# Expert weights fetched with two neighbouring rows per partition, and the features permuted to match

## The chip, the cores and the metric

The kernel runs on one core of one Trainium2 chip. The metric is the device time of one execution in microseconds; the median of three runs of the kernel before is 2015.76 us (2014.58 to 2028.83).

## What is computed

The reference is a two-layer backbone over 512 latent tokens and 256 context tokens of width 1024, all in float32. Each layer is a token mixer (an mLSTM in layer 0, a retention in layer 1) followed by a mixture of 16 experts. Everything is modulated by six vectors per layer that come from the condition `c` (shift, scale and gate of the mixer, shift, scale and gate of the experts). For this case the expert half matters:

```
h   = rmsnorm(x, norm_ffn_g[i]) * (1 + scale) + shift
aff = softmax(h @ router)                       # [tokens, 16]
gate, idx = top_k(aff.T, cap)                   # cap = 64 latent tokens, 32 context tokens
xs  = h[idx]
hid = silu(xs @ w_gate[e]) * (xs @ w_up[e])     # three 1024 x 1024 weights per expert
x  += gate_vector * scatter_add(idx, (hid @ w_down[e]) * gate)
```

Layer 0 does this for latent and context tokens, layer 1 for the latent tokens alone. The output is the latent stream after a final norm. The experts' weights of both layers are 2 x 16 x 3 matrices of 4 MB, about 403 MB of the 544 MB that the kernel reads.

## The kernel before

The kernel is one program written in a tile framework. A matrix product contracts over partitions: 1024 features are cut into 8 blocks of 128, and block k of the activations (the stationary operand, loaded into TensorE by a weight load) meets block k of the rows of the weights (the moving operand). In the traces "out<-moving,stationary" names them in this order.

**Expert weights.** `Route.load` (L1138 to L1158) brings 256 rows of a weight, 1 MB, into one slot of shape 128 x 2 x 1024: partition p holds row p and row p + 128 of the block, two pieces of 4 KB each. `Route.slot` hands out 19 slots or so in turn (four of a common pool and the pools that the mixer has left). All these loads are issued by SyncE's queue (SP), each as soon as the slot's last reader is done. `Route.prefetch` brings the first eight slots while the mixer's output projection runs. The last expert of layer 1 has its down weights in pieces of 2 KB.

**Experts.** `moe` runs over the experts: `gate_up` multiplies the chosen tokens `xs` with the gate weights and the up weights (PSUM tiles `gl` and `ul` for latent tokens, `cg` for context tokens), ScalarE and VectorE make the hidden values `hid` from them, `turn` (L1399) transposes `hid` with TensorE into `hp` and ScalarE copies it to `hT`, and `down` multiplies with the down weights into `y`. All products are in `prod` (L1260). `prep` and `prep_first` transpose the chosen tokens into `xs` (`xp`); in layer 1 they are picked by a product with one-hot columns (`xr`), and two experts are handled together and added back to the token tiles by a product (`back`).

**Vectors.** `ada_set`, `ada_set_lat` and `ada_columns` compute the modulation vectors as columns `modcol`, one feature block per column; `mk_gsc` makes the norm's scale from them; `rowbc` and `gate_rows` turn the mixer's gate and the experts' gate back into rows on all partitions. `mixer_end` does the output projection, the residual, the transposes `ht` of the new tokens (in `residual`, L942) and the router's product; `rt` holds the router's weights. At the start, small vectors are loaded as rows by ScalarE's queue and transposed into the columns `vc1` and `vc2`.

**Order.** The order of the instructions on each engine is not simply that of the program text. The framework's planner lays them out when the program is built, by its own estimates of how long each instruction and transfer takes, except where the code takes an engine out of its hands (`manual_schedule`, as for TensorE in the first and the last expert of layer 1). Once built, the order is fixed: an engine that waits for one instruction holds all that is queued behind it. The change touches no line that sets an order by hand.

Of the kernel before, what the change touches and what calls it, by code (L numbers as in the profile page):

```python
# [9 lines left out]
F32 = mybir.dt.float32  # L10
# [13 lines left out]
NE = 16  # L24
# [20 lines left out]
def backbone(ctx, tc, x, c, ctx_in, c_ctx, ada_w, ada_b, norm_mix_g, norm_ffn_g, final_norm_g,  # L45
# [29 lines left out]
    vc1 = consts.tile([128, 88], F32, name="vc1")  # L75
    vc2 = consts.tile([128, 96], F32, name="vc2")
    cst = consts.tile([128, 8, 32], F32, name="cst")
    with tc.tile_pool(name="ps0", bufs=1, space=PS, reuse_waits="tile") as ps0, \
            tc.tile_pool(name="rows0", bufs=1, reuse_waits="tile") as rows0:
        V = rows0.tile([128, 2, 128], F32, name="V")  # L80
        V1, V2 = V[:96, 0, :], V[:96, 1, :]
# [13 lines left out]
        rows(V1, 16, norm_ffn_g, 0, 16)  # L95
        rows(V1, 32, ada_b, 0, 48)
        rows(V1, 80, final_norm_g, 0, 8)
        rows(V2, 0, ada_b, 6 * D, 48)
        rows(V2, 48, conv_b, 0, 8)
        rows(V2, 56, conv_w, 0, 40)  # L100
        for V, n, vc in ((V1, 88, vc1), (V2, 96, vc2)):
            p = ps0.tile([128, 96], F32, name="pv", bufs=2)
            nc.tensor.transpose(p[:, :n], V[:n, :], ident[:n, :n])
            nc.vector.tensor_copy(vc, p[:, :n])
    conv_bc = vc2[:, 48:56]

    def conv_wc(w, ch):
        return vc2[:, 56 + w * 8 + ch:57 + w * 8 + ch]

    def adab(l):  # L110
        return vc1[:, 32:80] if l == 0 else vc2[:, 0:48]

# [6 lines left out]
    def ada_set(l, s, psp, sbp, wait=0):  # L119
        """modulation vectors 2 s and 2 s + 1 of layer l, both streams, as columns"""  # L120
# [10 lines left out]
    def ada_columns(l, s, acc, psp, sbp, streams, wait):  # L131
# [4 lines left out]
        for cc in range(4):  # L136
            nc.tensor.transpose(tp[:, cc, :], row[:, cc * 128:(cc + 1) * 128], ident)
        src = tp.rearrange("p c (q w) -> p q c w", w=32)
        for v in streams:
            nc.vector.tensor_tensor(modcol[l][:, s * 16:(s + 1) * 16, v].rearrange("p (q c) -> p q c", c=4),  # L140
                                    src[:, :, :, v],
                                    adab(l)[:, s * 16:(s + 1) * 16].rearrange("p (q c) -> p q c", c=4), op=OP.add)
# [5 lines left out]
    def ada_set_lat(l, s, psp, sbp, accs, wait):  # L148
        """ada_set for the latent stream alone; accs: two tiles [128, 1024] for the sums on every partition"""
# [19 lines left out]
    def ada_first(hh, psp, sbp):  # L169
        """shift and scale of the first mixer for half of the features; a column of the weights loaded third"""  # L170
# [18 lines left out]
        for v in range(2):  # L189
            dst, bias = [a.rearrange("p (m h c) -> p m h c", m=2, h=2)[:, :, hh]  # L190
                         for a in (modcol[0][:, 0:16, v], adab(0)[:, 0:16])]
# [5 lines left out]
    def hold(dst, col, eng=nc.gpsimd):  # L197
        """a load into dst starts after what col is read from has landed"""
        eng.tensor_copy(dst, col)

    def behind(late, early):
        """queues late, already emitted, behind early on their engine"""
# [6 lines left out]
    def mk_gsc(l, w, ks=slice(0, 8), vs=slice(0, 2)):  # L209
        g = vc1[:, 16 * w + 8 * l:8 + 16 * w + 8 * l]  # L210
# [10 lines left out]
    def rowbc(dst, l, m, v, psp):  # L221
        for hh in range(2):
# [4 lines left out]
            nc.scalar.activation(dst[:, hh * 512:(hh + 1) * 512], p.rearrange("p a b -> p (a b)"), AF.Copy)  # L227
# [31 lines left out]
    class Background:  # L259
        """instruction streams that are emitted between the matrix products of a projection"""  # L260
# [33 lines left out]
    def split_piece(wh, wl, w, eng=nc.vector):  # L294
        """w = wh + wl, both of them exact in the single-pass format"""
# [3 lines left out]
    class Proj:  # L299
        """hidden states of one mixer, transposed, in two parts, and the products with column blocks of weights"""  # L300
# [7 lines left out]
        def hidden(self, tiles, nx, held):  # L308
            """held: small loads that may wait until the first weights are there"""
# [164 lines left out]
    # ================= mixer of layer 0 =================  # L474
# [173 lines left out]
    def scan0(blk, sb, sp, pc, cols, flo, Y, gated):  # L648
        """four heads of the mLSTM, chunk by chunk, both directions; the incoming states are known"""
# [1191 lines left out]
```

## Time and profile before

| | |
|---|---|
| median of 3 runs | 2015.76 us (2014.58 to 2028.83) |
| profiled execution: span from the first to the last instruction | 2016.0 us; no time outside the span is given |
| TensorE busy | 1911.1 us, 95% of the span |
| VectorE, ScalarE, GpSimd busy | 724.5, 415.5, 275.2 us |
| moved by DMA | 585.42 MB, mean 290 GB/s |
| read from HBM | 544.13 MB |

The page shows one profiled execution. A matmul's record runs until its modelled end, so records overlap and a busy TensorE need not be a TensorE at its peak. "PEld" are the weight loads of TensorE, which run beside its matmuls. A queue's name with a q (SPq) stands for the issuing of a transfer or the waiting in that queue. The DMA share is the time that packets took, over 16 engines; it can exceed 1 a little. By time, the kernel has four stretches: the mixer of layer 0 to about 505 us, its experts to about 1077 us, the mixer of layer 1 to about 1475 us, and its experts to the end.

### The profile page before, as it was taken

The numbers are of one execution on the slowest core, as the hardware profiler recorded it, in microseconds if no ns is written. First come the engines' busy times: TensorE is split into PE (matmuls) and PEld (weight loads), VectorE is DVE, ScalarE is ACT, GpSimd is POOL, SyncE is SP. The second block draws the span as 40 slices with busy tenths as digits, with TensorE's granted clock in tenths as the row PEclk, the third lists the DMA queues.
The fourth block names the chain that finished last, engine by engine and source line by source line (L and its number), as shares of the span: only waits on it lengthen the run. The fifth ranks groups of instructions, "written<-read, shape, count | busy, mean of one in ns | idle before, by whom it ended". The sixth has DMA issues, their size and how long they took to land. (4 is left out here: it accounts for less than half of the span.)

```text
span 2016.0 us, 27905 instructions
## 1 busy us (share of the span) xinstructions
PE 1911.1 (95%) x11171; PEld 1021.4 (51%) x11171; DVE 724.5 (36%) x1766; ACT 415.5 (21%) x823; POOL 275.2 (14%) x331
## 2 busy tenths in 40 slices
PE   6999999999999999999998999998989999999997
PEld 2765776787344443333335877787743333333332
DVE  3544566556211111111105786265432212221223
ACT  3532454342000000000004523223310000000001
POOL 1111033201211121110012133143000000000001
PEclk9999999999999999999999999999989999999999
DMA  8568776563999999999975586455679999999981
GB/s 281 202 221 277 243 198 181 173 240 125 332 390 375 391 382 386 385 376 401 401 266 170 194 296 204 131 186 202 244 301 382 415 392 379 372 370 401 376 334 42
DMA packets 214226, 585.42 MB, mean 290 GB/s; under 512 B 17226, under 2 KB 64562, under 8 KB 208978
## 3 DMA queue, kind: packets, MB, share of 16 engines
q1 hardware_dynamic: 205808, 570.71, 76.5%
q0 software_dynamic: 6912, 12.71, 3.1%
q8 instruction: 88, 1.44, 0.3%
q10 hardware_dynamic: 1378, 0.23, 0.1%
q14 instruction: 40, 0.33, 0.0%
HBM read 544.13 MB, written 39.47 MB: 289 GB/s over the span
## 5 line engine op out<-in xcount | busy, mean ns | idle before, releaser
L1260 PE MATMUL y<-wslot,hT 128*32 128x256 f32 (+1 forms) x2016 | 291.7, 488 | 8.7 <-ACT hT L1405 8.4
L1260 PE MATMUL gl<-wslot,xs 128*64 128x512 f32 x1024 | 255.0, 604 | 0.8 <-DVE xs L1234 0.8
L1260 PE MATMUL ul<-wslot,xs 128*64 128x512 f32 x1024 | 240.1, 596 | 0.0
L290 PE MATMUL acc<-whi,hT_hi 128*128 128x512 f32 x544 | 223.7, 412 | 4.0 <-ACT hT_hi L360 3.1
L292 PE MATMUL acc<-whi,hT_lo 128*128 128x512 f32 x544 | 217.7, 401 | 0.2 <-DVE hT_lo L361 0.2
L291 PE MATMUL acc<-wlo,hT_hi 128*128 128x512 f32 x544 | 217.3, 400 | 0.0
L1260 PEld LDWEIGHTS y<-wslot,hT 128*32 128x32 f32 (+1 forms) x2016 | 100.1, 123 | 182.3 <-issue 145.5
L1397 DVE TENSOR_TENSOR hid<-hid,ul 128x512 f32<-128x512 f32 x32 | 22.0, 688 | 441.0 <-PE ul L1260 441.0
L1260 PEld LDWEIGHTS gl<-wslot,xs 128*64 128x64 f32 x1024 | 71.4, 137 | 147.9 <-issue 142.8
L1260 PEld LDWEIGHTS ul<-wslot,xs 128*64 128x64 f32 x1024 | 72.5, 137 | 142.1 <-issue 140.0
L1395 ACT ACTIVATE hid<-gl 128x512 f32<-128x512 f32 x32 | 19.1, 597 | 521.8 <-PE gl L1260 521.8
L290 PEld LDWEIGHTS acc<-whi,hT_hi 128*128 128x128 f32 x544 | 102.9, 189 | 39.1 <-issue 10.4
L1260 PE MATMUL cg<-wslot,xs 128*32 128x256 f32 x1920 | 118.9, 382 | 0.0
L292 PEld LDWEIGHTS acc<-whi,hT_lo 128*128 128x128 f32 x544 | 102.8, 189 | 29.0 <-issue 4.7
L291 PEld LDWEIGHTS acc<-wlo,hT_hi 128*128 128x128 f32 x544 | 103.0, 189 | 23.0 <-issue 2.4
L297 DVE TENSOR_TENSOR wlo<-wslot,whi 128x512 fp32r<-128x512 f32 x108 | 80.6, 762 | 57.5 <-ACT whi L296 57.2
L1260 PEld LDWEIGHTS cg<-wslot,xs 128*32 128x32 f32 x1920 | 56.5, 109 | 83.5 <-issue 51.1
L296 ACT ACTIVATE whi<-wslot 128x512 fp32r<-128x512 f32 x112 | 69.2, 629 | 97.8 <-PE acc L292 97.0
L1405 ACT ACTIVATE hT<-hp 128x512 f32<-128x512 f32 (+1 forms) x48 | 23.8, 524 | 293.1 <-PE hp L1403 293.1
L1357 POOL TENSOR_TENSOR xh<-x,wslot 128x512 f32<-128x512 f32 x4 | 5.0, 1276 | 523.6 <-issue 522.0
L290 PE MATMUL po<-woh,yh 128*128 128x512 f32 x160 | 65.2, 408 | 4.5 <-ACT yh L909 4.5
L291 PE MATMUL po<-wol,yh 128*128 128x512 f32 x160 | 65.3, 408 | 1.2 <-DVE wol L297 1.2
(429 smaller groups left out, 2411.9 us busy)
## 6 DMA issues: line engine op xcount, KB each, us to landing
wslot<-in_moe_w_up_dram SPq DMA_DIRECT2D x128, 1024.0 KB, 15.8
wslot<-in_moe_w_gate_dram SPq DMA_DIRECT2D x128, 1024.0 KB, 15.4
wslot<-in_moe_w_down_dram SPq DMA_DIRECT2D x124, 1024.0 KB, 13.3
wslot<-in_ada_w_dram SPq DMA_DIRECT2D x40, 1024.0 KB, 5.0
wslot<-in_ret_w_in_dram SPq DMA_DIRECT2D x16, 1024.0 KB, 7.6
wslot<-in_mlstm_w_in_dram SPq DMA_DIRECT2D x12, 1024.0 KB, 8.8
wslot<-in_ada_w_dram SPq DMA_DIRECT2D x16, 512.0 KB, 6.1
E<-rows_d SPq DMA_DIRECT2D x24, 256.0 KB, 5.8
```

What stands on the lines that cost most here:

```text
L290: nc.tensor.matmul(o, lh, rh, start=first, stop=False)
L291: nc.tensor.matmul(o, lh, rl, start=False, stop=False)
L292: nc.tensor.matmul(o, ll, rh, start=False, stop=last)
L296: nc.scalar.activation(wh, w, AF.Copy)
L297: eng.tensor_tensor(wl, w, wh.bitcast(F32), op=OP.subtract)
L1260: mm = nc.tensor.matmul(o[cw * q:cw * q + cw, :], stat(k), w(k)[:, qn * n:(qn + 1) * n], start=(k == 0), stop=(k == 7), tile_position=(0, ...
L1357: nc.gpsimd.tensor_tensor(O[:, lo], R.X[t][:, lo], fg[:, lo], op=OP.mult)
L1395: nc.scalar.activation(HID[v], o, AF.Silu)
L1397: nc.vector.tensor_tensor(HID[v], HID[v], o, op=OP.mult)
L1405: LATE["act"] = nc.scalar.activation(HT[v], p, AF.Copy)
```

## The change

Partition p of a slot now holds rows 2p and 2p + 1 of a block of 256 rows, one piece of 8 KB. Block k of a contraction therefore has the features 256 (k // 2) + 2 q + k % 2 in place of 128 k + q, and everything that meets these weights is put in the same order: the transposes of tokens and of hidden values read every second column, the router's weights and the vectors of the expert half (mixer gate, shift, scale, gate, the ffn norm's gain and the biases of these) are held in pair order, and the two places that make rows from such columns write every second element. The small vectors that are needed in pair order move from `vc1` and `vc2` into a third tile, loaded as rows of 256. The diff also drops comments and docstrings, which changes no instruction; those lines are left out here.

```diff
-    vc1 = consts.tile([128, 88], F32, name="vc1")
-    vc2 = consts.tile([128, 96], F32, name="vc2")
+    vc1 = consts.tile([128, 40], F32, name="vc1")
+    vc2 = consts.tile([128, 64], F32, name="vc2")
+    vcp = consts.tile([128, 40, 2], F32, name="vcp")
...
-        for V, n, vc in ((V1, 88, vc1), (V2, 96, vc2)):
-            p = ps0.tile([128, 96], F32, name="pv", bufs=2)
-            nc.tensor.transpose(p[:, :n], V[:n, :], ident[:n, :n])
+        for r0, src, off, n in ((0, norm_ffn_g, 0, 8), (8, ada_b, 2 * D, 16), (24, ada_b, 8 * D, 16)):
+            nc.scalar.dma_start(VP[r0:r0 + n, :], dram_ap(src, off, [[256, n], [1, 256]]))
+        for V, vc in ((V1, vc1), (V2, vc2), (VP[:, 0::2], vcp[:, :, 0]), (VP[:, 1::2], vcp[:, :, 1])):
+            n = V.shape[0]
+            p = ps0.tile([128, 64], F32, name="pv", bufs=2)
+            nc.tensor.transpose(p[:, :n], V, ident[:n, :n])
             nc.vector.tensor_copy(vc, p[:, :n])
...
+    def pairs_of(row):
+        return row.rearrange("p (b q j) -> p b j q", j=2, q=128)
...
         for cc in range(4):
-            nc.tensor.transpose(tp[:, cc, :], row[:, cc * 128:(cc + 1) * 128], ident)
+            cols = row[:, cc // 2 * 256 + cc % 2:cc // 2 * 256 + 256:2] if s else row[:, cc * 128:(cc + 1) * 128]
+            nc.tensor.transpose(tp[:, cc, :], cols, ident)
...
-            nc.scalar.activation(dst[:, hh * 512:(hh + 1) * 512], p.rearrange("p a b -> p (a b)"), AF.Copy)
+            nc.scalar.activation(pairs_of(dst[:, hh * 512:(hh + 1) * 512]),
+                                 p.rearrange("p (b j) q -> p b j q", j=2), AF.Copy)
...
-        nc.sync.dma_start(rt, router[l].rearrange("(k p) e -> p k e", p=128))
+        nc.sync.dma_start(rt.rearrange("p (b j) e -> p b j e", j=2),
+                          router[l].rearrange("(b p j) e -> p b j e", p=128, j=2))
...
-                nc.tensor.transpose(p[:, kk, :], XM[n][:, (b * 4 + kk) * 128:(b * 4 + kk + 1) * 128], ident)
+                c0 = b * 512 + kk // 2 * 256
+                nc.tensor.transpose(p[:, kk, :], XM[n][:, c0 + kk % 2:c0 + 256:2], ident)
...
-            nc.scalar.activation(M5[-1], p.rearrange("p a b -> p (a b)"), AF.Copy)
+            nc.scalar.activation(pairs_of(M5[-1]), p.rearrange("p (b j) q -> p b j q", j=2), AF.Copy)
...
-                                              [[D, 128], [128 * D, 2], [1, 512]]))
+                                              [[2 * D, 128], [D, 2], [1, 512]]))
             else:
-                nc.sync.dma_start(w, dram_ap((w_gate, w_up, w_down)[m], off + b * 256 * D,
-                                             [[D, 128], [128 * D, 2], [1, D]]))
+                nc.sync.dma_start(w.rearrange("p a c -> p (a c)"),
+                                  dram_ap((w_gate, w_up, w_down)[m], off + b * 256 * D, [[2 * D, 128], [1, 2 * D]]))
...
-                    ks = slice((hh * 4 + kk) * 128, (hh * 4 + kk + 1) * 128)
+                    k0 = hh * 512 + kk // 2 * 256
+                    ks = slice(k0 + kk % 2, k0 + 256, 2)
...
-                        nc.tensor.transpose(p[:, kk, :], rows_[:, kk * 128:(kk + 1) * 128], ident)
+                        nc.tensor.transpose(p[:, kk, :], rows_[:, kk // 2 * 256 + kk % 2:kk // 2 * 256 + 256:2], ident)
...
-                        nc.tensor.matmul(p[:, i, :], R.XH[t][:, k * 128:k * 128 + 128], pick[:, t, :],
+                        nc.tensor.matmul(p[:, i, :], R.XH[t][:, k // 2 * 256 + k % 2:k // 2 * 256 + 256:2], pick[:, t, :],
...
-                nc.tensor.transpose(p[:, cc, :], HID[v][:, cc * 128:(cc + 1) * 128], ident)
+                nc.tensor.transpose(p[:, cc, :], HID[v][:, cc // 2 * 256 + cc % 2:cc // 2 * 256 + 256:2], ident)
```

## Rows read from the trace of the kernel before

**Rows 1.** The page's first and second part: busy time of TensorE and its weight loads (with share of the span and instructions), then the DMA share in tenths in 40 equal slices of the span.

```profile
PE 1911.1 (95%) x11171; PEld 1021.4 (51%) x11171; DVE 724.5 (36%) x1766; ACT 415.5 (21%) x823; POOL 275.2 (14%) x331
...
DMA  8568776563999999999975586455679999999981
```

**Rows 2.** Busy time by stretch for the four stretches of the kernel. Columns: the stretch, its length, busy us (and instructions) of TensorE, weight loads, VectorE, ScalarE, GpSimd, then granted TensorE clock, DMA share, GB/s.

```profile
0.00:505.00 505.00, 474.06 (x2444) 334.45 (x2444) 271.71 (x744) 204.18 (x421) 83.61 (x154) 0.98 0.66 214
505.00:1077.00 572.00, 565.22 (x4783) 217.93 (x4783) 81.62 (x217) 35.91 (x74) 78.94 (x73) 1.00 0.98 361
1077.00:1475.00 398.00, 368.56 (x1947) 297.79 (x1943) 239.69 (x549) 135.40 (x255) 104.71 (x96) 0.98 0.63 216
1475.00:2016.00 541.00, 503.30 (x2002) 171.23 (x2002) 131.45 (x257) 40.02 (x73) 7.90 (x10) 0.99 0.87 342
```

**Rows 3.** The same view, expert by expert in layer 0: each stretch runs from one start of the product hid x ul on VectorE to the next. Seven experts lie between 564.69 and 805.29 us, six between 805.29 and 1030.42 us; columns as in rows 2.

```profile
564.69:599.05 34.36, 34.32 (x306) 14.46 (x302) 4.59 (x12) 1.85 (x4) 5.14 (x4) 1.00 1.03 385
...
770.70:805.29 34.59, 34.25 (x308) 13.89 (x304) 4.59 (x13) 1.85 (x4) 5.16 (x4) 1.00 1.03 384
...
919.39:956.50 37.11, 37.08 (x306) 12.62 (x302) 4.65 (x12) 1.85 (x4) 3.12 (x2) 1.00 1.03 398
...
993.62:1030.42 36.80, 36.77 (x306) 12.38 (x302) 4.04 (x9) 1.85 (x4) 3.11 (x2) 1.00 1.03 398
```

**Rows 4.** The same view, pair by pair of experts in layer 1, from the start of one pair's products `back` to the next. Four pairs lie between 1668.34 and 1933.97 us.

```profile
1543.70:1606.49 62.79, 60.16 (x243) 20.90 (x243) 15.23 (x28) 3.58 (x6) 0.00 (x0) 1.00 1.00 400
...
1668.34:1734.75 66.41, 62.22 (x243) 20.10 (x243) 15.05 (x28) 3.59 (x6) 0.00 (x0) 1.00 0.97 377
...
1867.56:1933.97 66.41, 62.22 (x243) 20.10 (x243) 14.87 (x27) 3.58 (x6) 0.00 (x0) 1.00 0.97 378
```

**Rows 5.** TensorE's instructions in order of time, inside an early expert and inside a late expert of layer 0. Columns: start, length of the run of records, line, product, how many.

```profile
684.64 7.08 PE L1260 MATMUL gl<-wslot,xs 128*64 128x512 f32 x30
691.65 3.66 PE L1260 MATMUL cg<-wslot,xs 128*32 128x256 f32 x64
...
865.88 1.94 PE L1260 MATMUL gl<-wslot,xs 128*64 128x512 f32 x8
867.75 1.07 PE L1260 MATMUL cg<-wslot,xs 128*32 128x256 f32 x16
```

**Rows 6.** What TensorE sat idle for ahead of the products of L1260, over the whole execution: us and times. Of this list, the entries that name a transfer of weights.

```profile
  DMA wslot<-in_moe_w_up_dram: 2.3, 6
  DMA wslot<-in_moe_w_gate_dram: 2.1, 5
  DMA wslot<-in_moe_w_down_dram: 1.5, 4
```

**Rows 7.** Transfers. First two stretches of the view of the slots' instructions: the SP queue's issues (ns min/median/max) and the time from issue to landing, in layer 0 (668 to 702 us) and in layer 1 (1734 to 1934 us). Then the page's line on packet sizes, the line of the modulation weights among the issues (1 MB each, 8 KB in one piece on a partition) with their median time to landing, and two stretches by time: one where such 8 KB pieces are the bulk (1202 to 1208 us) and the fullest one of 4 KB pieces in layer 1.

```profile
L1157 SPq DMA_DIRECT2D wslot<-in_moe_w_up_dram x4: 2244/2332/3157, 692.4 to 699.6; - x4
DMA to landing us min/median/max: 18.3/20.9/22.7
...
L1157 SPq DMA_DIRECT2D wslot<-in_moe_w_up_dram x24: 367/368/368, 1744.3 to 1932.5; - x24
DMA to landing us min/median/max: 6.6/8.5/11.3
...
DMA packets 214226, 585.42 MB, mean 290 GB/s; under 512 B 17226, under 2 KB 64562, under 8 KB 208978
...
wslot<-in_ada_w_dram SPq DMA_DIRECT2D x40, 1024.0 KB, 5.0
...
1202.00:1208.00 6.00, 6.00 (x31) 5.00 (x30) 6.00 (x11) 0.00 (x0) 3.84 (x2) 1.00 0.95 365
...
1510.00:1520.00 10.00, 10.00 (x50) 3.36 (x48) 0.67 (x1) 0.60 (x1) 0.00 (x0) 1.00 1.03 412
```

**Rows 8.** Weight loads of TensorE whose operand the change reads with a step of two, by line: count, ns min/median/max, first and last start. The last row is a load whose operand has step 0 (one column repeated 128 times).

```profile
L1403 PEld LDWEIGHTS hp<-ident,hid x160: 137/140/144, 524.5 to 1988.8; 128*128 128x128 f32 x160
...
L1222 PEld LDWEIGHTS xp<-ident,xg x144: 135/140/221, 503.1 to 1060.3; 96*128 96x128 f32 x112, 64*128 64x128 f32 x16, 32*128 32x128 f32 x16
...
L942 PEld LDWEIGHTS ht<-ident,xm x48: 138/140/144, 419.4 to 498.4; 128*128 128x128 f32 x48
...
L942 PEld LDWEIGHTS ht<-ident,x x32: 138/141/145, 1414.3 to 1460.8; 128*128 128x128 f32 x32
...
L1226 PEld LDWEIGHTS xp<-ident,rows x56: 138/140/143, 1528.0 to 1914.0; 128*128 128x128 f32 x56
...
L1245 PEld LDWEIGHTS xp<-pick,xh x64: 186/192/333, 1476.2 to 1492.2; 128*128 128x128 f32 x64
...
L225 PEld LDWEIGHTS rbp<-ident,modcol x24: 133/137/230, 400.4 to 1398.9; 128*128 128x128 f32 x24
```

**Rows 9.** Small work. ScalarE's copies of `rowbc`, VectorE's sums into `modcol` (which write every second element already), and at the start one of ScalarE's issues of small vectors and its first norm.

```profile
L227 ACT ACTIVATE mod<-rbp x6: 592/600/609, 407.9 to 1399.6; 128x512 f32<-128x512 f32 x6
...
L140 DVE TENSOR_TENSOR modcol<-adatp,vc x8: 164/172/177, 125.7 to 1220.3; 128x16 f32<-128x16 f32 x8
...
3.47 0.35 ACTq L85 DMA_DIRECT2D V<-in_mlstm_conv_w_dram  x1
...
7.22 1.06 ACT L233 ACTIVATE xjunk<-xt 128x1024 f32<-128x1024 f32 x1 [0.77 <-DMA xt<-in_x_dram]
```

**Rows 10.** TensorE at the start, in order of time: the first products with the modulation weights and what they waited for.

```profile
10.96 5.70 PE L181 MATMUL adaacc<-wslot,cst 128*32 128x512 f32 x16 [1.64 <-ACT xjunk L233]
```

More of the change, by code (lines that the diff above doesn't have):

```diff
@@ L80, in backbone @@
         V = rows0.tile([128, 2, 128], F32, name="V")
-        V1, V2 = V[:96, 0, :], V[:96, 1, :]
+        V1, V2 = V[:40, 0, :], V[:64, 1, :]
+        VP = rows0.tile([40, 256], F32, name="VP")
         Vc = rows0.tile([16, 128], F32, name="Vc")
@@ L94, in backbone, with adab @@
         rows(V1, 0, norm_mix_g, 0, 16)
[L95 to L100, printed above, removed]
-        for V, n, vc in ((V1, 88, vc1), (V2, 96, vc2)):
-            p = ps0.tile([128, 96], F32, name="pv", bufs=2)
-            nc.tensor.transpose(p[:, :n], V[:n, :], ident[:n, :n])
+        rows(V1, 16, ada_b, 0, 16)
+        rows(V1, 32, final_norm_g, 0, 8)
+        rows(V2, 0, ada_b, 6 * D, 16)
+        rows(V2, 16, conv_b, 0, 8)
+        rows(V2, 24, conv_w, 0, 40)
+        for r0, src, off, n in ((0, norm_ffn_g, 0, 8), (8, ada_b, 2 * D, 16), (24, ada_b, 8 * D, 16)):
[4 more added lines that the diff above has]
+            nc.tensor.transpose(p[:, :n], V, ident[:n, :n])
             nc.vector.tensor_copy(vc, p[:, :n])
-    conv_bc = vc2[:, 48:56]
+    conv_bc = vc2[:, 16:24]
     def conv_wc(w, ch):
-        return vc2[:, 56 + w * 8 + ch:57 + w * 8 + ch]
-    def adab(l):
-        return vc1[:, 32:80] if l == 0 else vc2[:, 0:48]
+        return vc2[:, 24 + w * 8 + ch:25 + w * 8 + ch]
+    def adab(l, s):
+        if s:
+            return vcp[:, 8 + 16 * l:24 + 16 * l].rearrange("p r j -> p (r j)")[:, (s - 1) * 16:s * 16]
+        return vc1[:, 16:32] if l == 0 else vc2[:, 0:16]
+    def pairs_of(row):
+        return row.rearrange("p (b q j) -> p b j q", j=2, q=128)
     modcol = [consts.tile([128, 48, 2], F32, name=f"modcol{l}") for l in range(2)]
@@ L141, in ada_columns @@
                                     src[:, :, :, v],
-                                    adab(l)[:, s * 16:(s + 1) * 16].rearrange("p (q c) -> p q c", c=4), op=OP.add)
+                                    adab(l, s).rearrange("p (q c) -> p q c", c=4), op=OP.add)
         if s == 0:
@@ L190, in ada_first @@
             dst, bias = [a.rearrange("p (m h c) -> p m h c", m=2, h=2)[:, :, hh]
-                         for a in (modcol[0][:, 0:16, v], adab(0)[:, 0:16])]
+                         for a in (modcol[0][:, 0:16, v], adab(0, 0))]
             nc.vector.tensor_tensor(dst, src[:, 0, :, :, v], bias, op=OP.add)
@@ L209, in mk_gsc @@
     def mk_gsc(l, w, ks=slice(0, 8), vs=slice(0, 2)):
-        g = vc1[:, 16 * w + 8 * l:8 + 16 * w + 8 * l]
+        g = vcp[:, 4 * l:4 * l + 4].rearrange("p r j -> p (r j)") if w else vc1[:, 8 * l:8 + 8 * l]
         m = 1 if w == 0 else 4
@@ L1322, in final_gain @@
                 for cc in range(4):
-                    nc.tensor.transpose(p[:, cc, :], vc1[:, 80 + h * 4 + cc:81 + h * 4 + cc].to_broadcast([128, 128]),
+                    nc.tensor.transpose(p[:, cc, :], vc1[:, 32 + h * 4 + cc:33 + h * 4 + cc].to_broadcast([128, 128]),
                                         ident)
```

## The prediction

> **What bounds the kernel now.** I read the page's busy times and its 40 slices first [rows 1]. TensorE is busy for 95% of the span, and the DMA share is at 9 tenths through two long stretches: these are the experts. Two resources are full at once there, and the question is which of them sets the pace. The view by stretch [rows 2] gives the sizes: 572 us for the experts of layer 0 with TensorE busy for 565.22 us, 541 us for those of layer 1 with 503.30 us. The mixers, 505 and 398 us, keep the DMA engines at 0.66 and 0.63.
>
> In layer 0 the transfers look like the limit. The DMA share is 1.03 [rows 3]; one issue on SP's queue takes 2.3 us where it takes 0.37 us in layer 1, and a weight block lands 20.9 us after its issue where it takes 8.5 us in layer 1 [rows 7]. The queue is choked. But look at TensorE by expert [rows 3]: 34.32 us busy of 34.36. The list of what TensorE waited for ahead of the expert products settles it: waits for weights come to 2.3 + 2.1 + 1.5 = 5.9 us in 15 waits over the whole execution [rows 6]. The transfers run at their limit, and they arrive in time all the same.
>
> So TensorE sets the pace, and its pace follows from the order of its instructions. Seven experts of layer 0 take (805.29 - 564.69) / 7 = 34.37 us each, the next six (1030.42 - 805.29) / 6 = 37.52 us, with the same number of matmuls [rows 3]. The timeline shows the difference [rows 5]: the early expert runs all of `gl` in one go, then all of `cg`; the late one changes between them after every block of weights. A whole `gl` takes 691.65 - 684.64 = 7.01 us in one go, and 4 x (867.75 - 865.88) = 7.48 us in four parts. The planner laid out the late experts as if each block of weights had only just come. In layer 1 it is the same by pairs: (1668.34 - 1543.70) / 2 = 62.32 us for the first two, (1933.97 - 1668.34) / 4 = 66.41 us for four later ones [rows 4].
>
> **The change, part by part.**
>
> *Expert loads.* 380 loads of 1 MB are issued as before, each with 128 pieces of 8 KB in place of 256 of 4 KB. No queue is passed and no wait is added. What a faster transfer can give is bounded by what TensorE waits for weights: 5.9 us [rows 6]. The waits sit ahead of weight loads, 0.4 us each, and weight loads run beside matmuls; I take a third, **-2 us**, and keep 0 and -6. What hides the transfers is 34.3 us of products per expert. If 8 KB pieces are slower, that cover gets thin, because in layer 0 nothing is spare. The nearest rows are the modulation weights, 8 KB in one piece already: where they are the bulk, 365 GB/s at a share of 0.95, or 384 at a full share, against 412 / 1.03 = 400 for 4 KB pieces [rows 7]. That is 4% less, and 0.04 x 34.4 x 16 = 22 us if layer 0 had to wait for all of it, 5 us more in the first two pairs of layer 1, which need 400 GB/s [rows 4]. That stretch also holds small transfers of the mixer, so I take no difference, and keep +27 us as the far end. What the choked SP queue gains (shorter issues) helps nobody: only the next weight load stands behind an issue.
>
> *Weight loads of TensorE with a step of two.* The transposes `hp` (160), `xp` (144 and 56), `ht` (48 and 32), 16 of the modulation columns and the 64 picks of `prep_first` keep their count and read every second column. They take 0.140 us each, the picks 0.192 us [rows 8]. No row shows a step of two. From below there is nothing to gain. From above, a load that reads half as fast takes twice as long: 456 x 0.140 + 64 x 0.192 = 76 us if all of it were exposed. The nearest row is the load with step 0, 137 ns [rows 8]: TensorE does not need neighbouring columns for its usual pace. I take **0**. [...]
>
> *Copies to rows.* Six copies of `rowbc` at 0.600 us [rows 9] and four of `gate_rows` of the same kind now write every second element. Doubled, they would cost 6 us; VectorE's sums into `modcol` write in such steps already, 172 ns for 16 elements [rows 9]. I take 0 and keep 0 to +6 us.
>
> *Start.* Two more issues on ScalarE's queue, 0.35 us each, stand ahead of its first norms; its second norm waited 0.77 us for tokens anyway [rows 9]. Two more small transposes and copies fall before 10.96 us, where TensorE had waited 1.64 us for ScalarE [rows 10]. Taken 0, at most +0.7 us. The router's weights come in pieces of 128 bytes in place of 64, twice in all: 0.
>
> *Order.* TensorE's queue is laid out anew by the planner. The products, their number and their sizes are the same, the transfers the same bytes. Where it starts to split the products depends on how long it thinks a load takes. That it split none before the eighth of these experts shows a price for a load only a little above what TensorE needs for it; I take that price to go by bytes, hence an unchanged order: 0, with the ends priced among the rivals.
>
> Sum against the profiled execution: 2016.0 - 2 + 0 = **2014 us**. Its span stands 0.2 us above the median of the runs, 2015.76 us, so nothing is corrected for that. The terms' small ends (-6, +6, +0.7) give this case a range of 2008 to 2023 us.
>
> **The rivals.**
>
> *The planner prices an 8 KB piece lower and stops splitting the products.* Then the late experts run like the early ones: 225.13 - 6 x 34.37 = 18.9 us in layer 0 and 265.63 - 4 x 62.32 = 16.4 us in layer 1 [rows 3, 4], together -35 us: 1980 us, or between that and 2014 if the splitting starts later but does start. For it: the order is the one thing that costs time here, and the loads are what it hangs on. Against: nothing in the change makes a load smaller. Its mirror, splitting from the first, costs 7 x (37.52 - 34.37) + 2 x 4.09 = 30 us: 2044 us.
>
> *Layer 0 hangs on its transfers after all.* For it: share 1.03, the choked queue [rows 3, 7]. If the stage went by transfers at 385 and 398 GB/s [rows 3] and 8 KB pieces held the best rate of 4 KB ones, 412 GB/s [rows 7], it would gain 240.6 x (1 - 385 / 412) + 225.1 x (1 - 398 / 412) = 15.8 + 7.6 = 23 us: 1991 us. Against: the experts' times agree within 0.3 us while the rate does not, and there are 5.9 us of waits. [...]
>
> *Strided weight loads are slower* (the slower side). They stand in TensorE's own queue, in front of `y` in every expert and of `xs`, four in a row, and nothing hides them. Doubled in full it is +76 us: 2090 us; half as much more, +38 us: 2052 us. It decides from 20 / 520 = 39 ns more per load, 180 ns in place of 140. For it: no row excludes it. Against: the row with step 0.
>
> That the pieces stay at 4 KB can be left out: 214226 - 208978 = 5248 packets have 8 KB or more, and the modulation weights' 40 x 128 = 5120 are among them [rows 7], so such a piece travels whole.
>
> **How the numbers follow.** The forecast gets 0.64, strided loads 0.12, the order without splitting 0.12, its mirror 0.06, transfers as the limit 0.06. I call a difference of over 1% (20 us) measurable. Faster by that: most of the order's gain (0.11) and of the transfers' (0.05), 0.16. Slower: strided loads above 39 ns (0.09) and most of the mirror or of slower pieces (0.05), 0.14. Within 1%: 0.70. The range reaches down to 1985, which takes in the transfers' case and most partial gains of the order, and up to 2038, which takes in slower pieces almost to their far end and strided loads up to 46 ns more; outside are a full gain of the order (0.05), heavier strided loads (0.08) and the mirror (0.04).
>
> **What would show it.** In the profile after: about 48640 packets fewer (380 x 128). Issues in layer 0 well below 2.3 us. Weight loads `hp`, `xp`, `ht` at 140 ns; if they stand at 180 or more, the strided rival is right. Experts of layer 0 at 34.4 us and later at 37 to 38 us, pairs of layer 1 at 62 and 66 us; if the step between them moves or goes, the order was laid out anew, and TensorE's timeline shows it in how often `gl` and `cg` change places. Waits for weights near 0; if they grow, 8 KB pieces are slower. The forecast is wrong if the time leaves 2008 to 2023 us with these rows unchanged.

## The result, and the profile after

The changed kernel takes 2031.81 us (median of 16 runs), the kernel before 2022.08 us in the runs beside it. The ratio is 1.0066, with a 95% interval of 1.0043 to 1.0088: slower by 8.7 to 17.8 us, 13 us in the middle. One of the 16 runs of the kernel before took 2215.12 us; the ratio goes by fast runs alone. The profiled execution spans 2034.9 us, 18.9 us more than before. That is more than the ratio gives, because single executions scatter with the clock that they are granted. Two runs of the kernel before show how much: 2013.75 us at a mean granted clock of 0.987 and 2030.73 us at 0.978. The two profiled executions stand at 0.982 (after) and 0.988 (before), and part of the difference lies in the mixers. So single spans are not compared below; stretches whose clock is shown are.

The page of the kernel after, as in [rows 1], and its line on packets, as in [rows 7]:

```profile
PE 1933.2 (95%) x11173; PEld 1048.0 (51%) x11173; DVE 725.9 (36%) x1768; ACT 416.0 (20%) x823; POOL 274.7 (13%) x331
...
DMA  7568765563999999999965585455579999999881
...
DMA packets 164546, 585.42 MB, mean 288 GB/s; under 512 B 16226, under 2 KB 63522, under 8 KB 110658
```

There are 214226 - 164546 = 49680 packets fewer: the 8 KB pieces travel whole. TensorE is busy for 22 us more, and so are its weight loads, by 27 us.

Weight loads of TensorE by tile in the kernel after; columns as in [rows 8]:

```profile
L1420 PEld LDWEIGHTS hp<-ident,hid x160: 194/209/223, 531.3 to 2007.8; 128*128 128x128 f32 x160
...
L1239 PEld LDWEIGHTS xp<-ident,xg x144: 191/216/223, 510.0 to 1072.8; 96*128 96x128 f32 x112, 64*128 64x128 f32 x16, 32*128 32x128 f32 x16
L1262 PEld LDWEIGHTS xp<-pick,xh x64: 193/196/196, 1490.3 to 1505.3; 128*128 128x128 f32 x64
L1243 PEld LDWEIGHTS xp<-ident,rows x56: 194/209/219, 1541.2 to 1931.0; 128*128 128x128 f32 x56
...
L958 PEld LDWEIGHTS ht<-ident,xm x48: 195/207/219, 425.6 to 505.2; 128*128 128x128 f32 x48
```

In the median, the transposing loads shown take 207 to 216 ns with the step of two where they took 140 [rows 8]. The loads of the picks, whose moving operand is not the identity, hardly change (192 to 196 ns).

What TensorE sat idle for ahead of the expert products, matmuls and weight loads together, the entries that name a transfer of expert weights (as in [rows 6]), and one row of SyncE's issues in the experts of layer 0 (676 to 710 us, as in [rows 7]):

```profile
  DMA wslot<-in_moe_w_up_dram: 6.7, 19
  DMA wslot<-in_moe_w_gate_dram: 5.4, 14
  DMA wslot<-in_moe_w_down_dram: 1.3, 4
```

```profile
L1173 SPq DMA_DIRECT2D wslot<-in_moe_w_up_dram x4: 328/328/328, 694.0 to 703.5; - x4
```

An issue takes 0.33 us where it took 2.3 us. But the waits for weights have grown, from 5.9 us in 15 waits to 13.4 us in 37. All of them stand ahead of weight loads; ahead of the matmuls themselves the list names no transfer in either kernel. The prediction took growing waits for the sign that 8 KB pieces are slower, so that rival has to be tested. The profile after gives no time from issue to landing for these transfers.

An early and a late expert of layer 0 and two pairs of layer 1 (columns as in [rows 2]; compare [rows 3, 4]):

```profile
572.27:606.88 34.61, 34.61 (x306) 15.89 (x302) 4.57 (x13) 1.85 (x4) 5.13 (x4) 1.00 1.02 392
...
930.11:967.56 37.45, 37.45 (x306) 13.14 (x302) 4.66 (x12) 1.85 (x4) 3.13 (x2) 1.00 1.02 409
```

```profile
1682.32:1749.09 66.77, 62.58 (x243) 20.60 (x243) 15.05 (x28) 3.58 (x6) 0.00 (x0) 1.00 0.93 372
1815.86:1884.32 68.46, 64.27 (x243) 21.00 (x243) 15.05 (x28) 3.58 (x6) 0.00 (x0) 0.98 0.93 375
```

An early expert is 0.24 us longer than before (34.37 us), a late one 0.34 us (37.11 us), a pair 0.36 us (66.41 us), and two pairs are 2.05 us longer. Those two have a granted clock of 0.98. The step from the early to the late pattern comes at the same expert as before. The instructions of every engine stand in the same order in both kernels, but for the start and one small GpSimd operation, so the order explains nothing.

Where an expert loses its time is seen in TensorE's instructions in order of time, around the transposes of an early expert. First the kernel before:

```profile
671.49 0.88 PE L1222 MATMUL xp<-ident,xg 96*128 96x96 f32 x8
672.20 1.05 PE L1403 MATMUL hp<-ident,hid 128*128 128x128 f32 x6
673.18 0.64 PE L1260 MATMUL gl<-wslot,xs 128*64 128x512 f32 x1
```

and the kernel after:

```profile
679.48 1.20 PE L1239 MATMUL xp<-ident,xg 96*128 96x96 f32 x8
680.51 0.96 PE L1420 MATMUL hp<-ident,hid 128*128 128x128 f32 x6
681.41 1.07 PE L1277 MATMUL gl<-wslot,xs 128*64 128x512 f32 x2
```

Take the starts, not the durations: eight `xp` need 672.20 - 671.49 = 0.71 us before and 680.51 - 679.48 = 1.03 us after. 0.32 us more on eight loads is 40 ns for each, not the 68 to 76 ns by which a load's duration grew. Loads and products overlap (TensorE busy for 95% of the span, its loads for 51%), and the pace counts. The six `hp` behind them take 0.98 us before and 0.90 us after: before, TensorE's weight loads waited 0.24 us ahead of the fifth, and the longer `xp` leave nothing of that wait. Both together, 1.69 us and 1.93 us, give the 0.24 us by which the expert is longer.

### The profile page after: what moved, and what is told of

Its sections match the earlier page's. It is cut to its first block, busy times and chain, and to the rows that moved or that the text cites. A ratio compares the mean times of both kernels' runs of the same rounds, so it can differ in the third digit from the quotient of the medians.

```text
span 2034.9 us, 27915 instructions
## 1 busy us (share of the span) xinstructions
PE 1933.2 (95%) x11173; PEld 1048.0 (51%) x11173; DVE 725.9 (36%) x1768; ACT 416.0 (20%) x823; POOL 274.7 (13%) x331
## 2 busy tenths in 40 slices
DMA packets 164546, 585.42 MB, mean 288 GB/s; under 512 B 16226, under 2 KB 63522, under 8 KB 110658
## 5 line engine op out<-in xcount | busy, mean ns | idle before, releaser
L1277 PEld LDWEIGHTS y<-wslot,hT 128*32 128x32 f32 (+1 forms) x2016 | 105.5, 123 | 179.7 <-issue 139.5
L304 PEld LDWEIGHTS acc<-whi,hT_hi 128*128 128x128 f32 x544 | 103.6, 190 | 39.2 <-issue 10.3
```

Source lines behind the costliest of these rows:

```text
L304: nc.tensor.matmul(o, lh, rh, start=first, stop=False)
L1277: mm = nc.tensor.matmul(o[cw * q:cw * q + cw, :], stat(k), w(k)[:, qn * n:(qn + 1) * n], start=(k == 0), stop=(k == 7), tile_position=(0, ...
```

## The experiments

Three theories were put against each other: the strided weight loads cost the time (1), the 8 KB pieces cost it (2), or it is a lower clock by chance (3). Two kernels take the change apart. `stride4k` is the kernel before with the step of two alone:

```diff
-                nc.tensor.transpose(p[:, cc, :], HID[v][:, cc * 128:(cc + 1) * 128], ident)
+                nc.tensor.transpose(p[:, cc, :], HID[v][:, cc // 2 * 256 + cc % 2:cc // 2 * 256 + 256:2], ident)
```

and so for `xp`, `ht`, the picks and the modulation columns. Expected:

> The kernel before with the step of two in the transposes hp, xp, ht, the picks and the modulation columns alone; the weights come in 4 KB pieces as before. It leaves out the match between features and weight rows. Theory 1 (strided weight loads): loads at 205 to 213 ns, ratio to the kernel before 1.004 to 1.009, an early expert of layer 0 at 34.6 us. Theory 2 (8 KB pieces): ratio 0.998 to 1.002 although the loads take 208 ns, because they run beside matmuls. Issues of SyncE's queue in layer 0 stay above 2 us in either case.

`contig8k` is the changed kernel with all of these read as neighbouring columns again:

```diff
-                nc.tensor.transpose(p[:, cc, :], HID[v][:, cc // 2 * 256 + cc % 2:cc // 2 * 256 + 256:2], ident)
+                nc.tensor.transpose(p[:, cc, :], HID[v][:, cc * 128:(cc + 1) * 128], ident)
```

> The changed kernel with the transposes reading neighbouring columns again; the 8 KB pieces stay. It leaves out the match between features and weight rows, so the experts and the router see features in the wrong order; every instruction and its place in its queue is that of the changed kernel. Theory 1 (the strided weight loads cost the time): loads hp, xp, ht back at 140 ns, an early expert of layer 0 at 34.37 us, ratio to the kernel before 0.998 to 1.002. Theory 2 (the 8 KB pieces cost it: they land late): loads at 140 ns, but the ratio stays at 1.004 to 1.009. Theory 3 (neither; the granted clock is lower in this kernel): the ratio follows the mean granted clock, about 1 us for each 0.0006 of it, whatever the loads do.

Measured: `stride4k` 1.0059 (1.0033 to 1.0086), `contig8k` 0.9998 (0.9971 to 1.0024). The step alone gives the whole effect, and the 8 KB pieces alone give none. Two stretches show it without the scatter of the mixers: 13 experts of layer 0 (from the second start of hid x ul to the fifteenth) and six pairs of layer 1 (from the first `back` on). First the kernel before, then after, `stride4k` and `contig8k`; columns as in [rows 2]:

```profile
564.69:1030.42 465.73, 463.79 (x3986) 178.80 (x3982) 61.44 (x161) 24.21 (x52) 62.34 (x48) 1.00 1.03 387
1543.63:1933.97 390.34, 368.10 (x1443) 120.81 (x1441) 90.27 (x167) 21.50 (x36) 0.00 (x0) 1.00 0.98 385
```

```profile
572.27:1042.33 470.06, 468.27 (x3986) 191.04 (x3982) 61.42 (x160) 24.10 (x52) 62.31 (x48) 1.00 1.02 389
1557.02:1952.78 395.76, 373.59 (x1443) 124.49 (x1441) 90.32 (x167) 21.51 (x36) 0.00 (x0) 0.99 0.94 382
```

```profile
563.67:1033.86 470.19, 468.40 (x3986) 189.94 (x3982) 61.27 (x161) 24.07 (x52) 62.37 (x48) 1.00 1.03 387
1548.44:1944.20 395.76, 373.60 (x1442) 124.51 (x1440) 90.28 (x167) 21.49 (x36) 0.00 (x0) 0.99 0.97 382
```

```profile
570.36:1035.80 465.44, 463.79 (x3986) 178.71 (x3982) 61.56 (x161) 24.07 (x52) 62.43 (x48) 1.00 1.02 392
1549.53:1939.89 390.36, 368.12 (x1442) 120.81 (x1440) 90.28 (x167) 21.49 (x36) 0.00 (x0) 1.00 0.95 385
```

`stride4k` repeats the kernel after to 0.13 us, and `contig8k` the kernel before to 0.3 us. Theories 2 and 3 fall. The longer waits for weights are no cost either: `contig8k` has them too, 12.6 us in 31 waits,

```profile
  DMA wslot<-in_moe_w_up_dram: 5.7, 12
  DMA wslot<-in_moe_w_gate_dram: 4.5, 11
  DMA wslot<-in_moe_w_down_dram: 2.4, 8
```

and its stretches are no longer than those of the kernel before. The loads wait, but no matmul of the experts does. In `stride4k` SyncE's queue stays choked (an issue of an up block takes 2390 ns, in the kernel after 328 ns), and this changes nothing: the 13 experts take 470.19 and 470.06 us.

**How the cost grows with the step.** `step4` is the changed kernel with a step of four in `xp`, `ht` and the `hp` of latent tokens:

```diff
-                nc.tensor.transpose(p[:, cc, :], HID[v][:, cc // 2 * 256 + cc % 2:cc // 2 * 256 + 256:2], ident)
+                nc.tensor.transpose(p[:, cc, :], HID[v][:, cc:HID[v].shape[1]:nb], ident)
```

> The changed kernel with a step of four float32 in place of two in the transposes hp (of latent tokens), xp and ht. It leaves out the match between features and weight rows. If any step other than one costs the same extra time, loads stay at 205 to 213 ns and the time equals that of the changed kernel (ratio to the kernel before 1.004 to 1.009). [...] By theory 2 (8 KB pieces) the ratio stays at 1.004 to 1.009 even with longer loads.

Measured: 1.0058 (1.0026 to 1.0090), as with the step of two, and loads of the same length:

```profile
L1418 PEld LDWEIGHTS hp<-ident,hid x160: 194/212/234, 521.6 to 2000.4; 128*128 128x128 f32 x160
```

From a step of two to one of four the load grows by 3 ns, from 209 to 212 in the median, where it grew by 69 from one to two. To see the pace by itself, `steps` ran transposes alone:

> A kernel by itself that computes nothing of the reference: groups of four transposes of float32 tiles, 128 and then 96 rows, with steps of 1, 2, 3, 4, 8 and 16 (tiles stepb, stepc, stepd, stepe, stepi, stepq), 16 of each, with long products between them that keep TensorE at its full clock. If a load has one slower pace for every step over one, all of 2, 3, 4, 8 and 16 take 195 to 215 ns at 120 to 123 ns from start to start, and step 1 takes 140 ns at 109 (128 rows) and 83 (96 rows). If the extra grows with the lines or bytes that the load spans, 8 and 16 are well above 4 (from 140 at step 1, 208 at 2 and 211 at 4, at least 10 ns more per doubling).

This run tells nothing about steps. In a kernel that does nothing else, TensorE ran at a pace of its own:

```profile
L68 PE MATMUL warm<-mov,ident 128*128 128x512 f32 x768 | 2035.4, 3027 | 6.6 <-DVE ident L56 6.6
```

Between two groups of transposes 48 products of this shape take 789.34 - 662.36 = 126.98 us, 2645 ns each, where eight `xr` of the same shape take 3.44 us in the kernel before, 430 ns each; with 128 rows 16 transposes take 662.36 - 651.78 = 10.58 us with the step of two and 799.92 - 789.34 = 10.58 us with that of three, 661 ns each, where 109 ns are usual (below). Both are slower by a factor of six. The views give a granted clock of 1.00, but that is no measurement: this trace holds no record of the clock at all, where that of the kernel before holds 16. Why TensorE was so slow was not found. So the same transposes were put into the kernel before, where TensorE is in its usual pace:

```diff
+                for rows in (128, 96):
+                    for s in (1, 2, 3, 4, 8):
...
+                        for i in range(16):
+                            nc.tensor.transpose(p[:, i % 4, :rows], R.XH[0][:rows, 0:127 * s + 1:s], ident[:rows, :rows])
```

> The kernel before with 160 transposes more at the start of the experts of layer 1, whose outputs go nowhere: steps of 1, 2, 3, 4 and 8 float32, 128 and then 96 rows, 16 of each (tiles stepafull to stephpart), in a kernel in which TensorE keeps its usual pace; it computes the same as the reference besides. If every step over one has the same pace, loads of steps 2, 3, 4 and 8 take 195 to 215 ns and follow each other at 120 to 123 ns, and those of step 1 take 140 ns at 109 (128 rows) and 83 (96 rows). If the extra grows with the span, step 8 stands at least 20 ns above step 2. The time rises by some 160 x 0.12 = 19 us, ratio 1.008 to 1.013; that is the length of what is added and decides nothing.

It took 2039.82 us in one run, beside 2031.32 us of the kernel before. TensorE's instructions in order of time (a, b, c, d, h stand for steps 1, 2, 3, 4, 8):

```profile
1481.14 1.91 PE L1446 MATMUL stepafull<-ident,xh 128*128 128x128 f32 x16
1482.89 2.08 PE L1446 MATMUL stepbfull<-ident,xh 128*128 128x128 f32 x16
1484.81 1.98 PE L1446 MATMUL stepcfull<-ident,xh 128*128 128x128 f32 x16
1486.62 2.09 PE L1446 MATMUL stepdfull<-ident,xh 128*128 128x128 f32 x16
1488.55 1.96 PE L1446 MATMUL stephfull<-ident,xh 128*128 128x128 f32 x16
1490.34 1.49 PE L1446 MATMUL stepapart<-ident,xh 96*128 96x96 f32 x16
1491.66 2.08 PE L1446 MATMUL stepbpart<-ident,xh 96*128 96x96 f32 x16
1493.58 2.03 PE L1446 MATMUL stepcpart<-ident,xh 96*128 96x96 f32 x16
1495.45 2.09 PE L1446 MATMUL stepdpart<-ident,xh 96*128 96x96 f32 x16
1497.37 1.94 PE L1446 MATMUL stephpart<-ident,xh 96*128 96x96 f32 x16
```

From one start to the next, over 16: with step 1 a transpose of 128 rows takes (1482.89 - 1481.14) / 16 = 109 ns, one of 96 rows (1491.66 - 1490.34) / 16 = 82 ns. The pace follows the columns of the product, 0.85 ns each. With step 2 it is (1484.81 - 1482.89) / 16 = 120 ns for 128 rows and (1493.58 - 1491.66) / 16 = 120 ns for 96: it no longer follows the product. Steps 3, 4 and 8 stand at 112 to 121 ns (the last row, 8 with 96 rows, has no next start of its kind), and 8 is no worse than 2, so the theory that the extra grows with the span falls. The loads take 194 to 209 ns with 128 rows and 217 to 236 ns with 96. What is read from this, and not shown by itself: behind neighbouring columns the product is the limit (109 and 82 ns), behind these steps the load is, at 112 to 121 ns. From step 1 to step 2 that costs a transpose of 128 rows 11 ns and one of 96 rows 38 ns.

**Which loads cost it.** In `xp_contig` only `xp` and the picks read neighbouring columns again, in `hp_contig` only `hp`:

```diff
-                    k0 = hh * 512 + kk // 2 * 256
-                    ks = slice(k0 + kk % 2, k0 + 256, 2)
+                    ks = slice((hh * 4 + kk) * 128, (hh * 4 + kk + 1) * 128)
```

> The changed kernel with only xp (of both layers, the picks among them) reading neighbouring columns again; hp, ht and the modulation columns keep the step of two. It leaves out the match between the tokens' features and the rows of gate and up weights. If the strided load is a limit only where its product is short: the 96-row transposes xp of layer 0 follow each other at 120 ns with the step and 83 without, 128 x 37 ns = 4.7 us, and those of layer 1 at 120 and 109, so this kernel loses 5 to 6 us of the 12 that the change costs: ratio to the kernel before 1.002 to 1.005. The two falls of the clock in the late pairs of layer 1 (3.4 us each at half the clock, 1.7 us of time each) stay if they come from hp. Rival: every strided load costs the same 0.068 us; then xp (200 loads and 64 picks of 456) carries under half and the ratio is 1.003 to 1.004 with hp_contig the same: the starts of xp and hp in the trace decide, not the ratio.

> The changed kernel with only hp reading neighbouring columns again; xp, ht, the picks and the modulation columns keep the step of two. It leaves out the match between hidden features and the rows of the down weights. If the strided load is a limit only where its product is short: hp gives back 160 x 11 ns = 1.8 us and up to 0.07 us at the first load of each of 48 groups, and with it the two falls of the clock in the late pairs of layer 1 (3.4 us together), if these come from the longer pause around hp: ratio 1.002 to 1.005, no fall of the clock between 1500 and 2000 us. If the falls stay, they come from xp or from scatter.

Measured: 1.0059 (1.0035 to 1.0083) and 1.0044 (1.0017 to 1.0071). The ratios don't separate the two, and that of `xp_contig` is above what was expected for it. The stretches separate them; first `xp_contig`, then `hp_contig`:

```profile
562.56:1028.92 466.36, 465.20 (x3986) 181.81 (x3982) 61.61 (x161) 24.07 (x52) 62.41 (x48) 1.00 1.02 391
1540.73:1937.23 396.50, 374.23 (x1442) 123.57 (x1441) 90.34 (x167) 21.49 (x36) 0.00 (x0) 0.99 0.94 381
```

```profile
576.44:1045.62 469.18, 467.27 (x3986) 188.13 (x3982) 61.41 (x160) 24.07 (x52) 62.26 (x48) 1.00 1.02 390
1557.62:1948.98 391.36, 369.18 (x1442) 122.12 (x1440) 90.33 (x167) 21.49 (x36) 0.00 (x0) 1.00 0.95 385
```

In layer 0 `xp` carries 470.06 - 466.36 = 3.7 us and `hp` 470.06 - 469.18 = 0.9 us, where 13 x 8 x 38 ns = 4.0 us and 13 x 6 x 11 ns = 0.9 us follow from the paces. In layer 1 `hp` carries 395.76 - 391.36 = 4.4 us and `xp` 391.36 - 390.36 = 1.0 us. By the paces, 6 x 8 x 11 ns = 0.5 us for each was to be expected. Most of the 4.4 us are not loads but clock. First a pair of the kernel before, around `hp`:

```profile
1857.57 0.66 PE L1403 MATMUL hp<-ident,hid 128*128 128x128 f32 x4 [0.86 <-DVE hid L1397]
1858.97 7.09 PE L1260 MATMUL y<-wslot,hT 128*64 128x512 f32 x32 [0.75 <-ACT hT L1405]
```

In the kernel after, in order of time inside the pair that begins at 1815.86 us, and by stretch:

```profile
1872.55 0.74 PE L1420 MATMUL hp<-ident,hid 128*128 128x128 f32 x4 [0.86 <-DVE hid L1414]
1874.04 8.78 PE L1277 MATMUL y<-wslot,hT 128*64 128x512 f32 x32 [0.75 <-ACT hT L1422]
```

```profile
1871.60:1874.90 3.30, 1.69 (x10) 0.90 (x10) 3.09 (x6) 0.60 (x1) 0.00 (x0) 1.00 1.01 415
1874.90:1878.40 3.50, 3.50 (x12) 1.01 (x10) 1.02 (x4) 0.00 (x0) 0.00 (x0) 0.51 1.01 426
```

From the start of `hp` to that of `y` it is 1.40 us before and 1.49 us after. Twelve times 0.09 us is 1.1 us, which is what `hp` costs in layer 1 without the falls (4.4 - 3.4 = 1.0 us). That is twice what the paces give. In these groups, ahead of which TensorE has waited, the second `hp` starts 221 ns after the first where it was 165, the next two follow after 120 each where it was 110. TensorE sat idle for 0.86 us ahead of `hp` and for 0.75 us behind it, as before; then the granted clock fell from 1.00 to about half, 0.51 over the 3.50 us shown, and `y` took 8.78 us where it took 7.09 before. Such a fall costs 68.46 - 66.77 = 1.7 us. The kernel after and `stride4k` have two of them in the six pairs (395.76 us, clock 0.99), `xp_contig` three (396.50 us, 0.99), `step4` three (397.55 us, 0.99); before, `contig8k`, `hp_contig` and `remedy` (below) have none (390.34 to 391.36 us, 1.00). `whole4k`, further below, has one without any step in `hp` (392.33 us). So the falls go with the step in `hp` but not with it alone, and with one profile of each kernel it is not shown that the longer pause brings them.

**The change without its cost.** `remedy` computes what the reference does with 8 KB pieces. The rows are put into halves where ScalarE and VectorE write them anyway, so `xp` and `hp` read neighbours:

```diff
-                nc.scalar.activation(HID[v], o, AF.Silu)
+                nc.scalar.activation(halves(HID[v]), pairs_of(o), AF.Silu)
             else:
-                nc.vector.tensor_tensor(HID[v], HID[v], o, op=OP.mult)
+                nc.vector.tensor_tensor(halves(HID[v]), halves(HID[v]), pairs_of(o), op=OP.mult)
```

> The changed kernel, computing the same as the reference, but the rows are de-interleaved where they are written: ScalarE's scaled copy of the tokens, its silu and VectorE's product hid x ul read every second element and write halves, so xp and hp read neighbouring columns; only ht and the modulation columns keep the step of two. Theory 1 (strided weight loads): ratio to the kernel before 0.998 to 1.003. Theory 2 (8 KB pieces): 1.004 to 1.009. Rival for this kernel: the strided reads make silu and product longer than 598 and 688 ns; they stand right before hp, so each 0.1 us more would cost up to 32 x 0.1 = 3 us, ratio 1.002 to 1.005.

Measured: 1.0002 (0.9975 to 1.0028); the 13 experts take 465.44 us, the six pairs 390.37 us. The strided reads of ScalarE and VectorE cost nothing that can be seen: in the 13 experts VectorE is busy for 61.55 us and ScalarE for 24.07, in `contig8k` for 61.56 and 24.07. Theory 1 is right again.

**Is the order what limits, as the prediction had it?** `whole4k` is the kernel before with TensorE's order in experts 1 to 14 of layer 0 written by hand, `whole8k` the same on `remedy`:

```diff
+                with tc.manual_schedule(engines={mybir.EngineType.PE}):
+                    gate_up(LAT, xs, 0, wg)
+                    gate_up(CTX, xs, 0, wg)
+                    gate_up(LAT, xs, 1, wu)
+                    gate_up(CTX, xs, 1, wu)
...
+                    turn(LAT)
+                    prep(e + 1, xn, streams if e + 2 < NE else (LAT,))
+                    turn(CTX)
+                    down(LAT, e, wd)
+                    down(CTX, e, wd)
```

> The kernel before (4 KB pieces, neighbouring columns) with TensorE's order in experts 1 to 14 of layer 0 written out by hand: all of gl, all of cg, all of ul, all of cg, hp of latent tokens, xp of the next expert, hp of context tokens, y. It computes the same as the reference. If TensorE's order alone makes the late experts slower (the reading in the prediction), all of them take 34.0 to 34.6 us and the ratio to the kernel before is 0.988 to 0.993 (6 x 3.15 = 19 us). If the transfers of 4 KB pieces set the pace there, waits for weights appear in the late experts and these stay above 36 us: ratio above 0.996.

> The kernel with 8 KB pieces and the rows de-interleaved where they are written (as in remedy), with the same order by hand in experts 1 to 14 of layer 0. It computes the same as the reference. If TensorE's order alone sets the pace, the ratio is that of whole4k, 0.988 to 0.993. If 4 KB pieces cannot keep up with the faster experts and 8 KB pieces can, this one is below whole4k by 0.3% or more, and its waits for weights are smaller: then the change has a use that the order hid.

Measured: 0.9894 (0.9859 to 0.9930) and 0.9887 (0.9847 to 0.9926). The stretch of the 13 experts, `whole4k` and then `whole8k`:

```profile
562.33:1000.19 437.86, 436.17 (x3930) 180.40 (x3926) 60.14 (x157) 25.51 (x52) 62.76 (x48) 1.00 1.03 386
```

```profile
567.13:1003.89 436.76, 435.64 (x3930) 180.71 (x3926) 60.14 (x156) 25.51 (x52) 62.77 (x48) 1.00 1.02 392
```

28 us come off 465.73, at the same DMA share (1.03 with 4 KB pieces, 1.02 with 8 KB): 33.6 us for every expert with 8 KB pieces, less than the 34.0 to 34.6 that were expected, because the early experts gain 0.8 us as well. With 4 KB pieces two experts are late (33.69 and 34.61 us), and matmuls wait for transfers (2.6 us in 5 waits); with 8 KB pieces none does. Ahead of weight loads the waits for weights are 10.3 us with 4 KB pieces and 5.0 us with 8 KB pieces.

`pipe4k` and `pipe8k` add a written order in layer 1, where the next expert's `gl` fills the pauses around `hp`, `hT` and `back`:

```diff
+                        gate_up(LAT, xs, 0, W[0], range(0, 4), e + 1)
+                        turn(LAT)
+                        gate_up(LAT, xs, 0, W[0], range(4, 8), e + 1)
+                        put_back(e, down_y(e, wd))
```

> whole4k (4 KB pieces, neighbouring columns, experts of layer 0 in a written order), and experts 0 to 13 of layer 1 also in a written order: the first half of the next expert's gl fills the time in which the hidden values are made, the rest the time of hT and of back. It computes the same as the reference. The products of a pair add to some 59 to 60 us, so if only the order sets the pace the pairs fall from 66.4 and 62.8 us to 59 to 61 us, ratio 0.972 to 0.980. Rival: at 24 blocks of 1 MB a pair, 60 us want 420 GB/s; the fullest stretch of 4 KB pieces gave 412. Then waits for weights appear and the pairs stand at 61 to 63 us, ratio 0.978 to 0.985.

> The same order on whole8k (8 KB pieces, de-interleaved where the rows are written). It computes the same as the reference. If the order alone sets the pace, the ratio is that of pipe4k within 0.2%. If transfers do, 8 KB pieces (426 GB/s in the fullest stretch of the changed kernel, against 412) give pairs of 59 to 61 us, 1 to 2 us below those of pipe4k, and 0.3 to 0.6% on the ratio, with fewer waits for weights: then the change is worth something once the order leaves the transfers no slack.

Measured: 1957.18 us, 0.9683 (0.9628 to 0.9739), and 1956.11 us, 0.9680 (0.9627 to 0.9733). Both beat both kernels by over 3%, and the ratios lie below the 0.972 to 0.980 that were expected of `pipe4k`. The six pairs, `pipe4k` and then `pipe8k`:

```profile
1521.86:1880.41 358.55, 354.59 (x1454) 129.75 (x1452) 90.14 (x167) 21.50 (x36) 0.00 (x0) 1.00 1.03 415
```

```profile
1526.15:1884.70 358.55, 354.58 (x1455) 129.75 (x1453) 90.12 (x167) 21.50 (x36) 0.00 (x0) 1.00 1.01 421
```

Both take 59.8 us a pair, and 4 KB pieces keep up at 415 GB/s; the rival that they would not falls. The 8 KB pieces show a lower DMA share for the same work (1.01, where 4 KB pieces have 1.03) and take away small waits of matmuls in layer 0 (3.2 us in 6). Between these two kernels that is not measurable.

## Why the prediction was wrong

*What bounds the kernel* was right and is now shown: TensorE's order sets the pace of the experts, and a better order gives 3.2%. Transfers run at a DMA share of 1.03 in the 13 experts of the kernel before and are hardly waited for (5.9 us in the whole execution). One line was misread: the early `gl` of [rows 5] counts 30 records of 32, since two stand ahead of `y`. The 7.01 us hold all the same: `whole4k` has all 32 in 786.71 - 779.69 = 7.02 us.

*Expert loads*: the term of -2 us came out at -0.3 us (465.73 to 465.44 in `contig8k`, with the pairs unchanged), and its ground, the waits for weights, does not hold. They grew, from 5.9 to 13.4 us (12.6 us in `contig8k`), which the prediction called the sign of slower pieces, and the time did not grow with them. Here a wait ahead of a weight load, beside a running product, was no price. The far end of +27 us for slower 8 KB pieces is excluded by `contig8k`. Pieces of 4 KB reach 415 GB/s (`pipe4k`) and those of 8 KB 421 GB/s (`pipe8k`) in stretches of the same length, 358.55 us.

*Weight loads with a step of two* is the step that failed: "I take 0". It rested on the nearest row, the load with step 0, and from that row it does not follow: a column repeated loads in 137 ns, columns at distances of 2, 3, 4 and 8 in 194 to 236 ns. A load went from 140 to 209 ns, above the 180 ns that were named as the sign of the rival. The rival was right that the loads take longer and wrong in price. For half as much more per load it had +38 us; 13 us came. The sentence "nothing hides them" is where it went wrong: loads overlap products (51% and 95% of the span), and what a step costs is the pace, 11 ns for 128 rows and 38 ns for 96, and not the 69 ns of duration; the first load of a group behind a wait costs more (221 - 165 = 56 ns in layer 1). On top of it come falls of the clock at 1.7 us each, which no term held. The stretches account for 4.3 us in layer 0 and 5.4 us in layer 1 (3.4 of them two falls), 9.7 of 13 us. The rest, `ht`, the experts outside of the stretches and scatter, was not taken apart. The step of two costs as much as the step of four: 1.0059 (`stride4k`) and 1.0058 (`step4`).

*Copies to rows*: 0.637 us in place of 0.600 for each `mod`, 0.2 us for six; 0.630 us in place of 0.597 for those of `gate_rows`. *Order*: unchanged, as forecast, and neither its rival nor the mirror came. *Start* was not separated from scatter.

The time lies inside the range (1985 to 2038 us), outside of the forecast case's own 2008 to 2023 us, and within 1%, on the slower side. That it is inside the range is luck: with loads longer by 69 ns the prediction's own price, 456 x 0.069 = 31 us, leads to 2045 us and out of the range. A load that was longer than thought and a price that was too high made up for each other.

## What to carry to other kernels

A permutation that a transfer wants has to be made where the data is read or written: put it into a copy that ScalarE or VectorE makes anyway, not into the operand that TensorE loads (here 1.0002 in place of 1.0066). Price a changed instruction by its pace from start to start among its like, and test one that no row shows by itself inside the kernel before it is taken as free. When an engine is busy all the time and its transfers are on time, look at the order of its instructions first; there the 3% were, and larger pieces had nothing to give in this kernel (`contig8k` 0.9998). A list of waits is not a list of costs: look whether a wait stands ahead of a product or of a load that runs beside one, where 13.4 us of waits cost nothing here.

## What was not expected of the hardware

The cost of a strided transposing load did not grow with the distance (steps 2 to 8: 112 to 121 ns from start to start). What a step of two cost went with the product beside the load: with one of 128 columns the pace grew by 11 ns, with one of 96 columns by 38 ns. A stretch around a pause of TensorE that grew by less than 0.1 us (`hp` 0.66 to 0.74 us, with 0.86 and 0.75 us of waiting around it in both kernels) came with falls of the granted clock from 1.00 to about half (0.51 over 3.50 us) that cost more than the loads themselves in layer 1 (3.4 of 5.4 us). Waits for weights ahead of weight loads more than doubled (5.9 to 13.4 us) without any cost. And TensorE alone, in a kernel with nothing else, was six times slower from start to start than in the full kernel (661 ns for a transpose in place of 109), in a trace without any record of the clock; this stays unexplained.
